# Weight sums on GpSimd and two residual chunks turned by DMA, in a two-layer decoder trunk

## The chip, the cores and the metric

One core of a Trainium2 chip runs one program. The metric is device time in microseconds (us) for one execution. The engines are named as the profile names them: PE is TensorE, DVE is VectorE, ACT is ScalarE, POOL is GpSimd and SP is SyncE, which here only starts DMAs. "L224" is line 224 of the kernel before the change.

## What is computed

Two layers over a residual stream `x` of 256 tokens by 2048 features in f32. Each layer has a mixer (differential attention in layer 0, latent attention in layer 1), a cross-attention into 256 memory tokens and a dense MLP. Each of them starts with an RMSNorm and ends with a plain add onto `x`.

```python
x = x + memory_cross_attention(rms_norm(x, cross_norm[i]), mem_h, ca_wq[i], ca_wkv[i], ca_wo[i])
x = x + sq_relu_mlp(rms_norm(x, mlp_norm[i]), mlp_wup[i], mlp_wdown[i])

def sq_relu_mlp(h, wup, wdown):        # wup 2048 x 8192, wdown 8192 x 2048
    return jnp.square(jax.nn.relu(h @ wup)) @ wdown
```

The change touches the two MLPs and the last step of each cross-attention, which feeds them.

## The kernel before the change

**Split weights.** Every f32 number is written as a high and a low part in the matmul's f32r format, and each product takes three matmuls: high by high, high by low, low by high. Activations stand still in the array and weights move through it, 512 columns at a time. A weight item is 1 MB (128 partitions by 2048 f32). It is loaded into one of seven buffers `raw`. Then it is split in two halves of 1024 columns: ACT casts the high part `whi` (L223), and DVE subtracts it to get the low part `wlo`, as `raw - whi` (L224). `whi` and `wlo` have four buffers each, so the split can be at most four halves ahead of PE.

**Blocks.** The 8192 hidden features fall into eight blocks of 1024. Block 0 of each MLP is computed plainly. Blocks 1 to 7 (the tuple `SEVEN`) are computed by class `Seven` with seven products p1 to p7 in place of eight: tokens, features and hidden columns are each cut in two, and sums of quarters of the activations are multiplied by sums of quarters of the weights. Each product has two items (`x` = 0 and 1), and an item of a product needs 12 matmuls, half of what an ordinary item needs (24, for both token halves). The order of the items in a block is p1 p1 p5 p5 p6 p3 p6 p3 p2 p7 p2 p7 p4 p4; at seven places in it an ordinary item of an earlier block's down-projection stands between them (`d` below): p1 p1 d p5 p5 d p6 d p3 p6 d p3 p2 d p7 p2 d p7 d p4 p4.

**Weight sums.** With quarters W11 to W22 of a block's weights, two buffers per `x` carry the running sums. `r["t", x]` is loaded with one quarter, and a DMA on POOL's queue that adds in flight (L961) puts W11 onto it when p1 runs. p1 itself uses W11 alone, p5 uses the sum. Before p6, DVE adds `r[22, x]` to it (L969, one instruction of 2048 columns). p3 uses `r[22, x]`; after its split a second adding DMA changes that buffer for p7. Before p2, DVE adds `r[21, x]` to `r["t", x]` (L969 again), which p4 uses last. So a block has four of these DVE adds, and the two MLPs have 56. A job's loads may be issued one job early: `fill` calls `fetch` of the job that is next in the plan.

**From the residual to the MLP.** `project_out` computes the cross-attention's output in four chunks of 512 features. For each chunk and token half, DVE adds the result onto `x` (L616), and `Forms.feed` makes the MLP's input from it: sum of squares (ACT), four 128x128 transposes on PE (`transpose4`, L176), multiplication by the norm's gain (DVE, L571), then a high and a low half (ACT L559, DVE L560). `FormUnit` tells PE's program which of these tasks an item waits for; before the change each unit waits for all tasks of its pair of chunks. The function `half_words` (ACT copy L392, store on POOL's queue L394) and `turned_by_dma` (DMA transpose on SP's queue, L399) are the other way to transpose, through DRAM; the norm ahead of each cross-attention uses it for chunks 0 and 1 already (`SENT`), as do the hidden blocks.

**Order of work.** PE's instructions stand in program order; the other engines' order is set by a planner in the compiler that simulates a timeline. `urgent()` gives work a higher priority in it, `behind(i)` puts an instruction after instruction `i`, and `keep_in_program_order` keeps DMAs in order. The helper tasks run on a clock of their own that counts PE's matmuls: a task's `yield T` means "go on when PE has worked T us more" (`T_SENT` 7.0, `T_BACK` 5.0, `T_ADD` 2.2).

Of the kernel before, what the change touches and what calls it, by code (L numbers as in the profile page):

```python
# [15 lines left out]
ALU = mybir.AluOpType  # L16
AX = mybir.AxisListType

P = 128
D = 2048  # L20
S = 256
NT = 2
CH = 512
# [5 lines left out]
SEVEN = (1, 2, 3, 4, 5, 6, 7)  # L29
# [5 lines left out]
T_EV, T_TURN, T_ROT, T_SM, T_SQ, T_ADD, T_NORM, T_SUM, T_BATCH, T_STORE, T_LAND, T_DMA, T_SHORT = 2.6, 2.6, 12.0, 6.5, 4.4, 2.2, 7.2, 3.0, 17.0, 22.0, 7.0, 8.0, 11.0  # L35

URGENT = 250
SENT = 0, 1
T_PART, T_JOIN, T_SENT, T_BACK = 5.0, 4.6, 7.0, 5.0
# [15 lines left out]
def trunk(ctx, tc, x, xT, xT0, mem, memT, positions, gcols, gfinal, lam_vecs, consts, W, out):  # L55
    nc = tc.nc
# [16 lines left out]
    def nm(s):  # L73
        serial[0] += 1
        return f"{s}_{serial[0]}"

    def unit():
        return units.tile([P, 2, 4, S], F32R, tag="unit", name=nm("unit"))
# [10 lines left out]
    class Task:  # L89
        def __init__(self, gen):  # L90
            self.gen = gen
            self.done = False
            self.waits = None
            self.ready = clock[0]
            self.serial = serial[0]
            side.append(self)
            self.step()
# [76 lines left out]
    def flip(o, src):  # L174
        clock[0] += 0.109
        nc.tensor.transpose(o, src, ident)  # L176

    def f32(ap):
        return ap.bitcast(F32)
# [3 lines left out]
    def behind(instruction):  # L183
        return tc.issue_after(instruction.ins) if instruction else nullcontext()

    def urgent():

        return tc.high_priority(offset=URGENT)
# [7 lines left out]
    def raw_tile():  # L196
        return wraw.tile([P, 4 * CH], F32, tag="raw", name=nm("raw"))
# [29 lines left out]
    def halves_of(raw, n=4 * CH, pieces=2):  # L227
        split = split_pieces(raw, n, pieces)
        for _ in range(pieces):
            split.next()  # L230
        return split.halves
# [158 lines left out]
    def half_words(src):  # L390
        planes = work.tile([P, 2, CH], U16, tag="ev", name=nm("planes"), padded_shape=[P, 2, CH], bufs=EVS)
        nc.scalar.copy(planes, src.bitcast(U16).rearrange("p (w s) -> p s w", s=2))  # L392
        there = turned.tile([2 * P, CH], U16, tag="turned", name=nm("turned"))
        nc.gpsimd.dma_start(there.rearrange("(q s) w -> q s w", s=2), planes)  # L394
        return there

    def turned_by_dma(there):
        landed = work.tile([P, 4, 2 * P], U16, tag="ev", name=nm("landed"), bufs=EVS)
        tc.keep_in_program_order(nc.sync.dma_start_transpose(landed, there))  # L399
        return landed.bitcast(F32).rearrange("p k t -> p k t")  # L400
# [29 lines left out]
    def transpose4(src, pt):  # L430

        for k in range(4):
            flip(pt[:, k * P : (k + 1) * P], src[:, k * P : (k + 1) * P])
        return pt.rearrange("p (k t) -> p k t", k=4)
# [25 lines left out]
    def sum_squares(acc, src, scale=1.0):  # L460
        junk = work.tile([P, CH], mybir.dt.bfloat16, tag="junk", name=nm("junk"), bufs=1)
        return nc.scalar.activation(junk[:, : src.shape[1]], src, AF.Square, scale=scale, accum_out=acc)  # L462
# [19 lines left out]
    class Stream:  # L482
# [8 lines left out]
        def feed(self, c, t, ps):  # L491
            if c not in self.units:
                self.units[c] = Held(unit())
            xc = xs[t][:, c * CH : (c + 1) * CH]

            def task():
                sum_squares(self.ss[t][:, c : c + 1], xc)
                yield T_ADD
                pt = transpose4(xc, ps)
                split(self.units[c], t, scaled(pt, g[:, self.gcol + 4 * c : self.gcol + 4 * c + 4]))  # L500
                yield T_TURN

            def unscaled():
                if c in self.sent:
                    with urgent():
                        there = half_words(xc)
                    yield T_SENT
                    pt = turned_by_dma(there)
                    yield T_BACK
                else:  # L510
                    yield T_ADD
                    pt = transpose4(xc, ps)
                split(self.units[c], t, pt)
                sum_squares(self.ss[t][:, c : c + 1], xc)
                yield T_TURN

            self.units[c].run(task() if self.sent is None else unscaled())
# [24 lines left out]
    class Forms(Stream):  # L542
# [2 lines left out]

        def __init__(self, gcol):
            super().__init__(gcol)
            self.raw = [raw_tile().rearrange("p (k t) -> p k t", t=P) for _ in range(NT)]
            self.forms = {}

# [11 lines left out]
        def feed(self, c, t, ps):  # L562
            xc = xs[t][:, c * CH : (c + 1) * CH]

            def task():
                sum_squares(self.ss[t][:, c : c + 1], xc)
                yield T_ADD
                pt = transpose4(xc, ps)
                rows = self.raw[t][:, 4 * c : 4 * c + 4]
                cols = g[:, self.gcol + 4 * c : self.gcol + 4 * c + 4]  # L570
                nc.vector.tensor_tensor(rows, pt, cols.unsqueeze(2).broadcast_to([P, 4, P]), ALU.mult)  # L571
                self.halves((t, c // 2), c % 2, rows)
                yield T_TURN

            self.form((t, c // 2)).run(task())

        def sum_of(self, key, inputs):

# [26 lines left out]
    class FormUnit:  # L605
        def __init__(self, forms, u):
            self.tiles = [forms.form((t, u // 2)) for t in range(NT)]
            self.at = 4 * (u % 2)
            self.tasks = [k for f in self.tiles for k in f.tasks]

        def get(self, half, kk, t):
            return self.tiles[t][:, half, self.at + kk]

    def add_residual(t, c, ps):
        xc = xs[t][:, c * CH : (c + 1) * CH]
        nc.vector.tensor_tensor(xc, xc, ps, ALU.add)  # L616


    def evacuate(ps, scale):
# [325 lines left out]
    class Seven:  # L945
# [20 lines left out]

        def job(self, p, x):
            def add(o, q):
                nc.vector.tensor_tensor(o, o, q, ALU.add)  # L969

            loads = {"p1": (("t", x), (0, 1)), "p6": ((22, x), (1, 1)), "p2": ((21, x), (1, 0))}

            def fetch():
                key, (i, j) = loads[p]
                if key not in self.raw:
                    home = f32(unit()).rearrange("p a k t -> p (a k t)") if p == "p1" and x == 0 and self.b < LAST - 2 else None
                    self.raw[key] = self.fetch(i, j, x, home=home)

            def run():
                r = self.raw  # L980
                if p in loads:
                    fetch()
                if p == "p1":
                    o = self.fetch(0, 0, x)
                    self.fetch(0, 0, x, r["t", x])
                elif p == "p5":
                    o = r["t", x]
                elif p == "p6":
                    o = r["t", x]
                    add(o, r[22, x])  # L990
                elif p == "p3":
                    o = r[22, x]
                    split = halves_of(o)
                    self.fetch(0, 1, x, o)
                    return split
                elif p == "p7":
                    o = r.pop((22, x))
                elif p == "p2":
                    o = r.pop((21, x))
                    add(r["t", x], o)  # L1000
                else:
                    o = r.pop(("t", x))
                return halves_of(o)

            if p in loads:
                run.fetch = fetch
            return run
# [260 lines left out]
    forms = {}  # L1268
# [45 lines left out]
    rows = ahead[:, 16 : 16 + 4 * S].rearrange("p (k t) -> p k t", t=S)  # L1314
# [144 lines left out]
    def project_out(acts_o, gcol):  # L1459
        nxt = Forms(gcol)  # L1460
        for c in range(4):
            ps = matmul_chunk(acts_o)
            for t in range(NT):
                add_residual(t, c, ps[t])
                nxt.feed(c, t, ps[t])
        return nxt

    def project_group(o, nxt=None, each=None):
        for c in range(4):
            ps = matmul_chunk([o])  # L1470
            if each:
                each(c)
            for t in range(NT):
                add_residual(t, c, ps[t])
                if nxt:
                    nxt.feed(c, t, ps[t])
# [248 lines left out]
    ps = matmul_chunk(acts, LAT)  # L1725
    latent_piece(eq, 0, ps, 0, LAT)
    ps = matmul_chunk(acts, LAT)
# [4 lines left out]
    ps = matmul_chunk(acts, 320)  # L1732
# [272 lines left out]
```

## Time and profile before the change

| What | Value |
|---|---|
| Time, median of 3 runs | 2160.42 us (2160.02 to 2160.5) |
| The profiled execution's own time | 2159.85 us |
| Its span, first to last instruction | 2158.1 us |
| PE busy | 2147.1 us, 99% |
| DVE busy | 1733.3 us, 80% |
| ACT busy | 1486.7 us, 69% |
| POOL busy | 225.4 us, 10% |
| Granted TensorE clock | 0.999 |

The span begins with the first instruction and ends with the last; the execution's own time has 1.75 us more around it. In a row of the groups, the numbers are the count, the busy time in us, the mean of one in ns, and the idle time of the engine just before such instructions with what ended it. In a row of the timeline they are the start, the length (of all instructions merged into the row) and how many there are.

### The profile page before, as it was taken

The page shows a single profiled execution, that of the slowest core. Times are in us where ns is not written, and L with a number is a line of the kernel's source. Part 1 is how long each engine was busy: PE and PEld are TensorE (multiplying, and loading weights), DVE is VectorE, ACT ScalarE, POOL GpSimd, SP SyncE. Part 2 cuts the span into 40 slices and gives each one's busy share as a digit, 9 for nine tenths or more (in the row PEclk, how much of TensorE's full clock was granted, in tenths as well). Part 3 has the DMA queues.
Part 4 walks back from the last instruction along what each step waited for, and adds up shares of the span by engine and source line. Part 5 has one row for each costly group of instructions (what it writes and reads, how often), then busy time and mean ns, then how long its engine had stood idle before and what let it go on. Part 6 is the DMA issues. An engine that isn't in the chain of part 4 may idle for free.

```text
span 2158.1 us, 27532 instructions
## 1 busy us (share of the span) xinstructions
PE 2147.1 (99%) x10109; PEld 1796.9 (83%) x10109; DVE 1733.3 (80%) x1962; ACT 1486.7 (69%) x1978; POOL 225.4 (10%) x354
## 2 busy tenths in 40 slices
PE   9999999999999999999999999999999999999998
PEld 7888888888888888888889988888888888888887
DVE  6576878788888889788886878778888888888887
ACT  7576656767777777776665765666777777777665
POOL 1123210001000000000000420000000000000001
PEclk9999999999999999999999999999999999999999
DMA  9678796748999999998986464665999999999995
GB/s 386 207 232 282 226 296 220 234 156 267 295 292 259 312 283 254 318 277 265 305 250 217 135 202 159 225 220 179 289 295 290 266 308 285 268 279 309 261 315 146
DMA packets 173944, 553.72 MB, mean 257 GB/s; under 512 B 100464, under 2 KB 100848, under 8 KB 114928
## 3 DMA queue, kind: packets, MB, share of 16 engines
q1 hardware_dynamic: 155136, 445.26, 58.6%
q0 software_dynamic: 18240, 105.92, 23.2%
q8 instruction: 79, 1.29, 0.2%
q10 hardware_dynamic: 432, 0.79, 0.1%
q14 instruction: 57, 0.47, 0.1%
HBM read 505.38 MB, written 24.12 MB: 245 GB/s over the span
## 4 chain that ended last, share of the span: by engine, by line
PE 96%; DVE 2%; DMA 1%; issue 1%; ACT 0%; DVEq 0%; POOLq 0%; POOL 0%
PE mm L172 63%; PE pr L172 28%; PE ax L172 3%; DMA raw<-in_mlp_wup_dram 1%; PE ax L176 1%; DVE wlo L224 1%; PE mm L176 1%; DVE raw L969 0%; DVE x L616 0%; DVE unit L428 0%; ACT whi L223 0%; PE ax L1326 0%; PE pr L176 0%; DVE unit L382 0%; DVE x L1875 0%
## 5 line engine op out<-in xcount | busy, mean ns | idle before, releaser
L224 DVE TENSOR_TENSOR wlo<-raw,whi 128x1024 fp32r<-128x1024 f32 (+3 forms) x930 | 1118.8, 1216 | 321.2 <-ACT whi L223 299.1
L223 ACT CAST whi<-raw 128x1024 fp32r<-128x1024 f32 (+3 forms) x929 | 968.2, 1044 | 541.6 <-PE mm L172 381.1
L172 PE MATMUL mm<-whi,unit 128*128 128x512 f32 (+2 forms) x4000 | 1268.9, 389 | 0.3
L172 PEld LDWEIGHTS mm<-whi,unit 128*128 128x128 f32 x4000 | 749.0, 188 | 148.9 <-DVE unit L382 1.1
L172 PE MATMUL mm<-wlo,unit 128*128 128x512 f32 (+2 forms) x2000 | 773.8, 387 | 0.2
L172 PE MATMUL pr<-whi,unit 128*128 128x512 f32 x1912 | 610.0, 389 | 0.0
L172 PEld LDWEIGHTS mm<-wlo,unit 128*128 128x128 f32 x2000 | 376.3, 188 | 73.6 <-DVE wlo L224 3.2
L172 PEld LDWEIGHTS pr<-whi,unit 128*128 128x128 f32 x1912 | 358.6, 188 | 73.4
L172 PE MATMUL pr<-wlo,unit 128*128 128x512 f32 x956 | 371.8, 389 | 0.4 <-DVE wlo L224 0.4
L172 PEld LDWEIGHTS pr<-wlo,unit 128*128 128x128 f32 x956 | 179.5, 188 | 39.2 <-DVE wlo L224 2.4
L394 POOL DMA_DIRECT2D turned<-planes x84 | 47.6, 567 | 732.2 <-ACT planes L392 706.6
L969 DVE TENSOR_TENSOR raw<-raw,raw 128x2048 f32<-128x2048 f32 x40 | 91.5, 2288 | 9.0 <-DMA raw<-in_mlp_wup_dram 8.8
L616 DVE TENSOR_TENSOR x<-x,mm 128x512 f32<-128x512 f32 x128 | 85.2, 682 | 15.2 <-PE mm L172 15.1
L961 POOL DMA_DIRECT2D raw<-in_mlp_wup_dram x48 | 43.4, 905 | 448.0 <-DVE wlo L224 425.7
L468 POOL TENSOR_TENSOR rs<-rs,mhalf 128x1 f32<-128x1 f32 (+1 forms) x26 | 21.7, 837 | 385.7 <-DVE rs L467 385.6
L224 DVE TENSOR_TENSOR wlo<-unit,whi 128x1024 fp32r<-128x1024 f32 x48 | 57.3, 1221 | 5.3 <-ACT whi L223 4.0
L223 ACT CAST whi<-unit 128x1024 fp32r<-128x1024 f32 x48 | 49.8, 1054 | 9.8 <-PE pr L172 9.8
L392 ACT COPY planes<-p 128x1024 uint16<-128x1024 uint16 x48 | 50.0, 1041 | 0.3
L172 PE MATMUL mm<-unit,whi 128*128 128x256 f32 x256 | 46.7, 284 | 0.0
L462 ACT ACTIVATE junk<-x 128x512 bf16<-128x512 f32 (+1 forms) x57 | 35.3, 619 | 11.0 <-DVE x L1174 5.2
L1539 ACT ACTIVATE p<-p,r 128x512 f32<-128x512 f32 x42 | 30.4, 724 | 15.3 <-DVE p L1044 7.4
L172 PEld LDWEIGHTS mm<-unit,whi 128*128 128x128 f32 x256 | 40.2, 192 | 0.3
(207 smaller groups left out, 1314.3 us busy)
## 6 DMA issues: line engine op xcount, KB each, us to landing
raw<-in_mlp_wdown_dram SPq DMA_DIRECT2D x128, 1024.0 KB, 7.2
raw<-in_mlp_wup_dram SPq DMA_DIRECT2D x120, 1024.0 KB, 7.0
raw<-in_mlp_wup_dram POOLq DMA_DIRECT2D x48, 1024.0 KB, 9.0
raw<-in_da_wqkv_dram SPq DMA_DIRECT2D x45, 1024.0 KB, 8.6
turned<-planes POOLq DMA_DIRECT2D x84, 256.0 KB, 6.1
raw<-in_da_wo_dram SPq DMA_DIRECT2D x16, 1024.0 KB, 8.2
raw<-in_ca_wkv_dram SPq DMA_DIRECT2D x16, 1024.0 KB, 7.6
raw<-in_mlp_wdown_dram POOLq DMA_DIRECT2D x16, 1024.0 KB, 10.2
```

The costliest lines, as they stand in the source:

```text
L172: return nc.tensor.matmul(o, stationary, moving, start=start, stop=stop, skip_group_check=onto)
L176: nc.tensor.transpose(o, src, ident)
L223: nc.scalar.copy(hi, r)
L224: nc.vector.tensor_tensor(lo, r, f32(hi), ALU.subtract)
L392: nc.scalar.copy(planes, src.bitcast(U16).rearrange("p (w s) -> p s w", s=2))
L394: nc.gpsimd.dma_start(there.rearrange("(q s) w -> q s w", s=2), planes)
L462: return nc.scalar.activation(junk[:, : src.shape[1]], src, AF.Square, scale=scale, accum_out=acc)
L468: nc.gpsimd.tensor_tensor(r[:, :n], r[:, :n], mhalf.broadcast_to([P, n]), ALU.pow)
L616: nc.vector.tensor_tensor(xc, xc, ps, ALU.add)
L961: tc.keep_in_program_order(nc.gpsimd.dma_start(onto, src, accum_op=ALU.add))
L969: nc.vector.tensor_tensor(o, o, q, ALU.add)
L1539: nc.scalar.activation(r, src, AF.Relu, scale=rstd[t])
```

## The change

Part 1 moves the weight sums. `add` goes from DVE, in one instruction of 2048 columns, to GpSimd, in two of 1024. The sum ahead of p6 is issued when the quarter `r[22, x]` is fetched, one job earlier than before. In the first block that uses the seven products (block 1 of each MLP), the sum for p5 is no longer made by an adding DMA from DRAM; GpSimd adds the W11 that p1 has loaded anyway.

Part 2 concerns the residual chunks 0 and 1 ahead of each MLP. They are transposed through DRAM in place of PE, with an order hint that keeps the multiplication by the gain behind the latest residual add, and `FormUnit` waits only for its own chunk's tasks.

```diff
@@ class Forms @@
+            self.turning = {}
@@ feed @@
             def task():
+                if c in SENT:
+                    with urgent():
+                        there = half_words(xc)
                 sum_squares(self.ss[t][:, c : c + 1], xc)
-                yield T_ADD
-                pt = transpose4(xc, ps)
+                if c in SENT:
+                    yield T_SENT
+                    pt = turned_by_dma(there)
+                    yield T_BACK
+                else:
+                    yield T_ADD
+                    pt = transpose4(xc, ps)
                 rows = self.raw[t][:, 4 * c : 4 * c + 4]
                 cols = g[:, self.gcol + 4 * c : self.gcol + 4 * c + 4]
-                nc.vector.tensor_tensor(rows, pt, cols.unsqueeze(2).broadcast_to([P, 4, P]), ALU.mult)
+                with behind(c in SENT and latest[0]):
+                    nc.vector.tensor_tensor(rows, pt, cols.unsqueeze(2).broadcast_to([P, 4, P]), ALU.mult)
                 self.halves((t, c // 2), c % 2, rows)
                 yield T_TURN

-            self.form((t, c // 2)).run(task())
+            form = self.form((t, c // 2)).run(task())
+            self.turning[t, c] = form.tasks[-1]
@@ class FormUnit @@
-            self.tasks = [k for f in self.tiles for k in f.tasks]
+            self.tasks = [forms.turning[t, u] for t in range(NT)]
@@ add_residual @@
-        nc.vector.tensor_tensor(xc, xc, ps, ALU.add)
+        latest[0] = nc.vector.tensor_tensor(xc, xc, ps, ALU.add)
@@ Seven.job @@
             def add(o, q):
-                nc.vector.tensor_tensor(o, o, q, ALU.add)
+                for at in (slice(0, 2 * CH), slice(2 * CH, 4 * CH)):
+                    nc.gpsimd.tensor_tensor(o[:, at], o[:, at], q[:, at], ALU.add)
@@ fetch @@
                     self.raw[key] = self.fetch(i, j, x, home=home)
+                    if p == "p6":
+                        add(self.raw["t", x], self.raw[22, x])
@@ run @@
                 if p == "p1":
                     o = self.fetch(0, 0, x)
-                    self.fetch(0, 0, x, r["t", x])
+                    if self.b == SEVEN[0]:
+                        add(r["t", x], o)
+                    else:
+                        self.fetch(0, 0, x, r["t", x])
...
                 elif p == "p6":
                     o = r["t", x]
-                    add(o, r[22, x])
```

More of the change, by code (lines that the diff above doesn't have):

```diff
@@ L608, in __init__ @@
             self.at = 4 * (u % 2)
-            self.tasks = [k for f in self.tiles for k in f.tasks]
+            self.tasks = [forms.turning[t, u] for t in range(NT)]
         def get(self, half, kk, t):
             return self.tiles[t][:, half, self.at + kk]
+    latest = [None]
     def add_residual(t, c, ps):
         xc = xs[t][:, c * CH : (c + 1) * CH]
-        nc.vector.tensor_tensor(xc, xc, ps, ALU.add)
+        latest[0] = nc.vector.tensor_tensor(xc, xc, ps, ALU.add)
     def evacuate(ps, scale):
```

## The prediction

> **What bounds the kernel now.** First the page: engine shares and the chain that ended last, then the DVE groups with shapes kept apart, then the waits of PE's weight loads.
>
> ```profile
> span 2158.1 us, 27532 instructions
> PE 2147.1 (99%) x10109; PEld 1796.9 (83%) x10109; DVE 1733.3 (80%) x1962; ACT 1486.7 (69%) x1978; POOL 225.4 (10%) x354
> PE 96%; DVE 2%; DMA 1%; issue 1%; ACT 0%; DVEq 0%; POOLq 0%; POOL 0%
> ```
> ```profile
> L969 DVE TENSOR_TENSOR raw<-raw,raw 128x2048 f32<-128x2048 f32 x40 | 91.5, 2288 | 9.0 <-DMA raw<-in_mlp_wup_dram 8.8
> L969 DVE TENSOR_TENSOR unit<-unit,raw 128x2048 f32<-128x2048 f32 x16 | 36.6, 2288 | 0.8 <-DMA raw<-in_mlp_wup_dram 0.6
> ```
> ```profile
> PEld mm L172 <- DVE wlo L224: 3.2, 8, 0.5
> PEld pr L172 <- DVE wlo L224: 2.4, 5, 0.6
> ```
>
> PE is the bound: it idles 2158.1 - 2147.1 = 11.0 us in all, and its loads waited 3.2 + 2.4 = 5.6 us for DVE's low parts. So a time below this one can come only from work taken off PE, or from those few us. The 56 sums hold DVE for 91.5 + 36.6 = 128 us, yet PE hardly waits for it. What decides about part 1 is thus not DVE's share but how far the splits run ahead of PE. That is seen in one block of layer 1: PE's side from the chain in order of time, DVE's and ACT's from the timeline.
>
> ```profile
> 1582.72 2.72 PE pr L172 x12
> ...
> 1607.20 5.44 PE pr L172 x24
> 1612.64 5.44 PE mm L172 x24
> 1618.08 2.72 PE pr L172 x12
> 1620.80 5.44 PE mm L172 x24
> 1626.24 5.44 PE pr L172 x24
> 1631.68 5.44 PE mm L172 x24
> 1637.12 5.44 PE pr L172 x24
> ```
> ```profile
> 1602.33 2.36 DVE L224 TENSOR_TENSOR wlo<-unit,whi 128x1024 fp32r<-128x1024 f32 x2 [0.67 <-ACT whi L223]
> 1604.72 2.29 DVE L969 TENSOR_TENSOR unit<-unit,raw 128x2048 f32<-128x2048 f32 x1
> 1606.93 1.22 DVE L224 TENSOR_TENSOR wlo<-raw,whi 128x1024 fp32r<-128x1024 f32 x1
> 1608.32 2.59 DVE L224 TENSOR_TENSOR wlo<-raw,whi 128x1024 fp32r<-128x1024 f32 x2 [0.17 <-ACT whi L223]
> 1610.82 2.28 DVE L969 TENSOR_TENSOR raw<-raw,raw 128x2048 f32<-128x2048 f32 x1
> 1613.02 1.22 DVE L224 TENSOR_TENSOR wlo<-raw,whi 128x1024 fp32r<-128x1024 f32 x1
> ...
> 1625.78 2.28 DVE L969 TENSOR_TENSOR unit<-unit,raw 128x2048 f32<-128x2048 f32 x1
> 1627.98 3.49 DVE L224 TENSOR_TENSOR wlo<-raw,whi 128x1024 fp32r<-128x1024 f32 x3
> 1631.38 2.29 DVE L969 TENSOR_TENSOR raw<-raw,raw 128x2048 f32<-128x2048 f32 x1
> ...
> 1637.66 2.36 DVE L224 TENSOR_TENSOR wlo<-raw,whi 128x1024 fp32r<-128x1024 f32 x2
> ```
> ```profile
> 1611.31 1.05 ACT L223 CAST whi<-unit 128x1024 fp32r<-128x1024 f32 x1 [0.30 <-PE pr L172]
> ```
>
> A product's item is 2.72 us on PE (12 matmuls), a `d` item 5.44, a block 14 x 2.72 + 7 x 5.44 = 76.2 us. A half of a product's item is 1.36 us on PE, and its low part 1.13 us on DVE (three in 3.49, the last of them 1.22). ACT waits for PE to give a buffer back, so the splits cannot run further ahead than the four buffers. PE's row at 1607.20 is p5 p5, 1612.64 `d`, 1618.08 p6, 1620.80 `d`, 1626.24 p3 p6, 1631.68 `d`, 1637.12 p3 p2. The pair of low parts at 1637.66 is p2's: the first ends near 1638.8 and PE wants it at 1639.84 plus one matmul, 1640.1, so only 1.3 us is in hand. For p6's second half (the second low part of a product after 1625.78, done at 1629.2, wanted at 1630.5) it is also 1.3 us.
>
> **Part 1: the sums on POOL.** Removed: 56 DVE instructions of 2.29 us. Added: 60 sums (56, and two in each MLP's first block) of two instructions each, 120 on POOL. The trace of before has the same form at a quarter of the width, once with DVE beside it, and smaller ones in layer 1's mixer:
>
> ```profile
> 2135.95 3.46 DVE L224 TENSOR_TENSOR wlo<-raw,whi 128x1024 fp32r<-128x1024 f32 x2
> 2136.34 1.99 POOL L1896 TENSOR_TENSOR x<-x,unit 128x512 f32<-128x512 f32 x1 [17.56 <-ACT junk L462]
> ```
> ```profile
> 1200.75 0.46 POOL L635 TENSOR_TENSOR rope<-ev,sin 128x128 f32<-128x128 f32 x1
> ```
> ```profile
> 1200.77 1.52 DVE L224 TENSOR_TENSOR wlo<-raw,whi 128x1024 fp32r<-128x1024 f32 x1 [0.30 <-ACT whi L223]
> ```
>
> Two low parts that follow each other take 2.36 us at 1602.33 and 3.46 us here: 1.10 us longer, next to a POOL instruction that began 0.39 us into the first of them and ran 1.99. The reading that fits: POOL waited 0.8 us for the first low part to end, then ran 1.15 us while the second stood still. At 1200.77 one low part took 1.52 in place of 1.22 beside a 128x128 one of 0.46. So the two engines exclude each other, and 384 more columns cost 1.10 - 0.30 = 0.80 us, 2.1 ns each. A half sum of 1024 columns then holds DVE for 1.10 + 512 x 2.1 ns = 2.2 us, the whole sum for 4.4, against 2.2 that DVE spent itself (2.29 less the overlap). **The change does not free DVE; it takes 2.2 us more of its time per sum.** The lower end for a half is 2.0 us (with 3.46 - 2 x 1.22 = 1.02 in place of 1.10), the upper end 4.0 (twice the whole 1.99). No exclusion at all at this width is one of the rivals, since no row shows 1024 columns.
>
> The Trainium skill, "SBUF — State Buffer", section "Who interferes with whom", has the rule: a DVE instruction with two SBUF inputs contends with a GpSimd instruction that reads SBUF, and whoever starts first has the port for the whole instruction. The 1.10 us above agree; by that rule DVE's residual adds, with one input in PSUM, would go on beside a sum, and the sum below would come out lower by what share of them meets one. The "GPSIMD Engine Reference", section "Elementwise — side-by-side cycle accounting", gives 4497 ns for an add of 2048 f32, so 2.25 us for a half by that page, which would put 0.1 us more on each sum and some 4 us on the forecast.
>
> What lies in the lead and what reaches PE, walked through the block above. p6's first sum can start when p5's split is done, at 1604.7. POOL 1604.7 to 1606.9; low part 1606.9 to 1608.1, as before; POOL 1608.1 to 1610.3; low part to 1611.4, wanted at 1611.5. The next one, for `d`, runs to 1612.5 (wanted 1612.8). p6's second sum has been ready since 1611.4: POOL to 1614.7, low part to 1615.8, wanted at 1615.6, PE is 0.2 late; POOL to 1618.0, low part of p6 to 1619.1, wanted at 1618.3 + 0.2, 0.6 later still. The p6 pair costs PE 0.8 us. In the p2 pair each sum costs 2.2 us more than before where 1.3 was in hand: 0.9 each, 1.8. Together 2.6 us a block; 14 blocks give 36 us. Between the ends: nothing, if lead recovered elsewhere covers it, and 56 x 2.2 = 123 us, if all the excess reaches PE. I take the walk.
>
> The sums themselves arrive in time: 4.4 us plus two waits of 1.2 is 6.8 us, and the pieces they feed come later (p6's cast at 1611.31 needs only the first half, done at 1606.9; p2's pair at 1637.66 is 11.9 us after its sum's old start). Behind a waiting sum on POOL's queue stand the stores for the hidden blocks and p3's adding DMA.
>
> ```profile
> L961 POOL DMA_DIRECT2D raw<-in_mlp_wup_dram x48: 863/887/1261, 487.2 to 2016.9; - x48
> ...
>   ACT whi L223: 9.4, 5
> ...
> DMA to landing us min/median/max: 7.9/9.5/17.5
> ```
>
> Those adding DMAs were waited for 9.4 us in all; p3's lands 7.9 to 17.5 us after its issue, and p7's split comes an item or two later still. I cost the delay at nothing; without that cover it would be up to 6.8 us for a DMA, and the time would go to the third rival's. In an MLP's first block, two sums of 4.4 us come on top where an adding DMA cost DVE nothing: 2 x 4.4 against leads of 1.3 to 2.6; I take 2 us per MLP, 4 in all, ends 0 and 18. Four adding DMAs (and 4 MB) go, worth at most those 9.4 us, and by count 4 in 48 of them, 0.8: nothing.
>
> **Part 2: chunks 0 and 1 by DMA.** PE loses 2 chunks x 2 halves x 4 transposes = 16 per MLP. Their price is the distance of two chunks in the chain: 6.33 us, with 24 matmuls of 5.44 in it.
>
> ```profile
> 462.40 5.46 PE mm L172 x24
> 468.73 5.49 PE mm L172 x24
> ```
>
> Eight transposes cost 6.33 - 5.44 = 0.89 us; four times that, 3.6 us, leaves PE's own time and so the path. Added: 8 ACT copies, 8 stores on POOL, 8 transposing DMAs on SP. The same path in the cross-attention ahead shows what it costs:
>
> ```profile
> 399.31 0.39 PE L172 MATMUL mm<-wlo,unit 128*128 128x512 f32 x1
> 399.84 0.73 PE L172 MATMUL mm<-whi,unit 128*128 128x512 f32 x2
> ```
> ```profile
>   PEld mm L172: 0.6, 1
> ...
> DMA to landing us min/median/max: 3.3/3.3/4.7
> ```
> ```profile
> 455.00:482.00 27.00, 27.00 (x137) 22.68 (x136) 22.87 (x33) 18.86 (x32) 0.00 (x0) 1.00 0.52 189
> ```
>
> There the first unit is wanted three chunks after its rows were added, as here, and PE was 0.3 us late once (399.84 against 399.54). The stretch ahead of the MLP has its DMAs at 0.52 and ACT busy 18.9 of 27.0 us, so four copies near 1 us fit. If that cover were gone, SP's transposes would wait and hold up the weight loads behind them. I take 0.3 us per MLP, 0.6; ends 0 and 3 each.
>
> **Sum.** 2159.85 (this execution) - 3.6 + 36 + 4 + 0.6 = 2196.9; the runs' median is 0.57 above this execution, so 2197.4, +1.7%.
>
> **The rivals.** *The excess is absorbed* (the other side): DVE is idle a fifth of the span, and if the planner or the wait for p2's quarter moves the POOL halves next to `d` items, whose halves are 2.72 us on PE, the lead covers them. It decides where less than 1.3 us of a sum's excess falls between two product items. Then only part 2 counts: 2160.42 - 3.6 + 0.6 = 2157.4, -0.14%. For it: PE waited 5.6 us in all so far. Against it: 1.3 us in hand, 2.2 taken. *The engines do not exclude each other at this width*: DVE gains 128 us, the 5.6 us of waits go too: 2157.4 - 5.6 = 2151.8, -0.4%. Against it are the 3.46 and 1.52 us rows. *The delays pile up*: each late half moves the next sum into a shorter lead, and nothing is won back; twice the walk, 5.2 us a block: 2197.4 + 36 + 4 = 2237. That the change does less than it says is no case here: 16 transposes go in each MLP whatever else happens.
>
> **Chances and range.** The walk or a like size 0.57, piled up 0.20, absorbed 0.14, no exclusion 0.09. About 0.2% (4.3 us) is what a measurement of this kernel can tell from no change. Absorbed falls mostly within it (0.11 of 0.14, the rest faster): faster 0.12, same 0.11, slower 0.77. The walk's own range is 2175 to 2222 (1.2 to 4 us a block). Leaving out 0.09 below and about 0.1 above, the range is 2156 to 2238.
>
> **What would show it.** POOL's sums at 2.2 to 3.5 us each and low parts (L224) with a mean above 1.23 us, many near 3.4; waits of PE's loads for L224 grown from 5.6 to about 40 us, mostly at p6, p3 and p2; PE busy down 3.6 us in transposes; no wait for `landed` at the MLPs' start over 1 us. If L224 keeps its mean, the exclusion is wrong; if it grows and PE does not wait, the lead was larger than I read.

## The result and the profile after

| | before | after |
|---|---|---|
| Time, median | 2160.46 us (2160.02 to 2160.71) | 2271.01 us (2269.36 to 2273.0) |
| Ratio | | 1.0513, 95% interval 1.0498 to 1.0527 |
| Profiled execution | 2159.85 us | 2269.89 us (span 2268.1) |

The change made the kernel 110.6 us slower. The forecast was 2197.4 us, with a range up to 2238: the direction was right, the size was not. The page of the changed kernel, with the rows that answer to those of before (L983 is the sum, on POOL now):

```profile
span 2268.1 us, 27674 instructions
PE 2179.0 (96%) x10077; PEld 1791.6 (79%) x10077; DVE 1839.9 (81%) x1906; ACT 1492.1 (66%) x1986; POOL 590.7 (26%) x478
PE 72%; DVE 16%; issue 7%; ACT 2%; DMA 2%; SPq 0%; POOL 0%; DVEq 0%; POOLq 0%; ACTq 0%
L224 DVE TENSOR_TENSOR wlo<-raw,whi 128x1024 fp32r<-128x1024 f32 (+3 forms) x930 | 1329.7, 1446 | 330.7 <-ACT whi L223 312.4
L983 POOL TENSOR_TENSOR raw<-raw,raw 128x1024 f32<-128x1024 f32 x84 | 263.2, 3170 | 38.4 <-DMA raw<-in_mlp_wup_dram 23.3
L983 POOL TENSOR_TENSOR unit<-unit,raw 128x1024 f32<-128x1024 f32 x36 | 106.0, 3012 | 56.8 <-DMA raw<-in_mlp_wup_dram 35.5
```

The low parts' row of before reads:

```profile
L224 DVE TENSOR_TENSOR wlo<-raw,whi 128x1024 fp32r<-128x1024 f32 (+3 forms) x930 | 1118.8, 1216 | 321.2 <-ACT whi L223 299.1
```

DVE lost 128 us of sums and is still busy 106.6 us longer, because its low parts stretched (1329.7 - 1118.8 = 211 us). The chain that ended last gives PE 72% in place of 96%, and DVE 16% in place of 2%; in the block shown below its longer pieces of "issue" lie inside low parts that stand still. The waits of PE's weight loads say the same; before, the first two rows were 3.2 and 2.4 us:

```profile
PEld mm L172 <- DVE wlo L224: 70.9, 59, 4.3
PEld pr L172 <- DVE wlo L224: 41.7, 42, 2.3
PEld mm L172 <- DVE unit L561: 6.5, 3, 2.7
```

By the distances between the first matmuls of successive p1 products, a regular block took 76.16 us before and 83.2 after. Against before, 46.0 us are lost in MLP 0's seven blocks and 46.7 in MLP 1's. The stretches ahead of the two MLPs' first such block lost 7.9 and 9.5 more.

One block of layer 1 shows how. From the timelines of DVE, POOL and PE (a row of DVE or POOL merges instructions that follow each other, with their count at the end):

```profile
1675.77 2.42 DVE L224 TENSOR_TENSOR wlo<-raw,whi 128x1024 fp32r<-128x1024 f32 x1 [0.91 <-ACT whi L223]
1678.49 9.72 DVE L224 TENSOR_TENSOR wlo<-raw,whi 128x1024 fp32r<-128x1024 f32 x3 [0.30 <-ACT whi L223]
...
1697.66 16.30 DVE L224 TENSOR_TENSOR wlo<-raw,whi 128x1024 fp32r<-128x1024 f32 x6 [1.54 <-ACT whi L223]
```
```profile
1673.81 6.65 POOL L983 TENSOR_TENSOR unit<-unit,raw 128x1024 f32<-128x1024 f32 x2 [1.34 <-DVE wlo L224]
1680.42 6.71 POOL L983 TENSOR_TENSOR raw<-raw,raw 128x1024 f32<-128x1024 f32 x2
1697.11 0.89 POOL L974 DMA_DIRECT2D raw<-in_mlp_wup_dram  x1 [9.98 <-issue]
1697.73 5.05 POOL L983 TENSOR_TENSOR unit<-unit,raw 128x1024 f32<-128x1024 f32 x2
1703.95 6.66 POOL L983 TENSOR_TENSOR raw<-raw,raw 128x1024 f32<-128x1024 f32 x2 [1.17 <-DVE wlo L224]
```
```profile
1684.92 0.50 PE L172 MATMUL mm<-wlo,unit 128*128 128x512 f32 x1 [1.68 <-DVE wlo L224]
1688.27 0.50 PE L172 MATMUL mm<-wlo,unit 128*128 128x512 f32 x1 [0.31 <-DVE wlo L224]
1703.92 0.50 PE L172 MATMUL pr<-wlo,unit 128*128 128x512 f32 x1 [1.76 <-DVE wlo L224]
1708.40 0.50 PE L172 MATMUL mm<-wlo,unit 128*128 128x512 f32 x1 [1.44 <-DVE wlo L224]
1711.75 0.50 PE L172 MATMUL mm<-wlo,unit 128*128 128x512 f32 x1 [0.31 <-DVE wlo L224]
```

p6's two sums (1673.81 and 1680.42) run without a gap: four halves, 3.3 us each. Beside them the three low parts at 1678.49 need 9.72 us, one per 3.2 us, where they took 3.49 before; PE wants one per 1.36 us in a product and per 2.72 us in a `d` item. In p2's first sum (1697.73) both halves take 5.05 us together, not 6.7: DVE got no turn between them, and the low part that began at 1697.66 ended at 1703.87, 6.2 us later. p2's second sum goes in turns again. PE stood 1.68 + 0.31 us behind p6's pair and 1.76 + 1.44 + 0.31 us behind p2's, 5.5 us. The distances of the matmuls' starts are the better measure, since the matmul after a wait is followed 0.34 us later in place of 0.23: by them the two pairs cost 2.8 and 4.4 us, nearly all of the 7.3 us by which this block is longer. In 10 of the 14 blocks p2's first sum goes as it does here; in the first and the last of each MLP's seven it goes in turns.

### The profile page after: what moved, and what is told of

The parts are those of the page before. It is cut to its first block, busy times and chain, and to the rows that moved or that the text cites. A ratio compares the mean times of both kernels' runs of the same rounds, so it can differ in the third digit from the quotient of the medians.

```text
span 2268.1 us, 27674 instructions
## 1 busy us (share of the span) xinstructions
PE 2179.0 (96%) x10077; PEld 1791.6 (79%) x10077; DVE 1839.9 (81%) x1906; ACT 1492.1 (66%) x1986; POOL 590.7 (26%) x478
## 4 chain that ended last, share of the span: by engine, by line
PE 72%; DVE 16%; issue 7%; ACT 2%; DMA 2%; SPq 0%; POOL 0%; DVEq 0%; POOLq 0%; ACTq 0%
PE mm L172 49%; PE pr L172 20%; DVE wlo L224 12%; PE ax L172 2%; ACT whi L223 1%; DMA landed<-turned 1%; DVE unit L561 1%; PE ax L176 1%; DVE x L629 1%; DVE raw L599 1%; DVE raw L581 0%; DVE unit L382 0%; DVE wlo L243 0%; ACT planes L392 0%; PE mm L176 0%
## 5 line engine op out<-in xcount | busy, mean ns | idle before, releaser
L224 DVE TENSOR_TENSOR wlo<-raw,whi 128x1024 fp32r<-128x1024 f32 (+3 forms) x930 | 1329.7, 1446 | 330.7 <-ACT whi L223 312.4
L223 ACT CAST whi<-raw 128x1024 fp32r<-128x1024 f32 (+3 forms) x929 | 967.4, 1043 | 581.7 <-PE mm L172 398.1
L172 PE MATMUL mm<-wlo,unit 128*128 128x512 f32 (+2 forms) x2000 | 782.8, 392 | 46.8 <-DVE wlo L224 46.1
L172 PE MATMUL pr<-wlo,unit 128*128 128x512 f32 x956 | 376.5, 394 | 24.8 <-DVE wlo L224 24.7
L983 POOL TENSOR_TENSOR raw<-raw,raw 128x1024 f32<-128x1024 f32 x84 | 263.2, 3170 | 38.4 <-DMA raw<-in_mlp_wup_dram 23.3
L394 POOL DMA_DIRECT2D turned<-planes x92 | 52.2, 567 | 795.8 <-ACT planes L392 780.4
L983 POOL TENSOR_TENSOR unit<-unit,raw 128x1024 f32<-128x1024 f32 x36 | 106.0, 3012 | 56.8 <-DMA raw<-in_mlp_wup_dram 35.5
L224 DVE TENSOR_TENSOR wlo<-unit,whi 128x1024 fp32r<-128x1024 f32 x48 | 57.2, 1218 | 5.6 <-ACT whi L223 5.5
L1103 POOL DMA_DIRECT2D raw<-in_mlp_wdown_dram x16 | 13.9, 872 | 170.8 <-DVE wlo L224 134.6
L223 ACT CAST whi<-unit 128x1024 fp32r<-128x1024 f32 x48 | 49.6, 1051 | 13.3 <-PE pr L172 13.3
L172 PE MATMUL mm<-unit,whi 128*128 128x256 f32 x256 | 46.7, 284 | 0.0
```

Source lines behind the costliest of these rows:

```text
L172: return nc.tensor.matmul(o, stationary, moving, start=start, stop=stop, skip_group_check=onto)
L223: nc.scalar.copy(hi, r)
L224: nc.vector.tensor_tensor(lo, r, f32(hi), ALU.subtract)
L983: nc.gpsimd.tensor_tensor(o[:, at], o[:, at], q[:, at], ALU.add)
```

## The experiments

All changes are against the kernel before, unless said. Ratios are against runs of the kernel before on the same chip.

### The two parts alone

Part 1 alone is the diff's `Seven.job`; part 2 alone is the rest.

> Part 1 alone on the kernel before (sums on GpSimd, the first block's sum too; all residual chunks still turned on PE). Theory (GpSimd's sums hold DVE's two-input work): the blocks cost as much as in the changed kernel, about 93 us, and some 5 us more come ahead of the first blocks, 2255 to 2262 us. Rival (the two parts hurt each other, mainly at the MLPs' starts): under 2240 us.

> Part 2 alone on the kernel before (chunks 0 and 1 turned by DMA, sums on DVE). By the prediction's own step: -3.6 + 0.6, 2157.5 us. By what the changed kernel's trace shows ahead of its MLPs (PE waits 2.4 and 0.9 us for the last chunks' rows, and the matmuls behind a long wait run at 427 ns): 2160 to 2168 us.

Part 1 alone: 2265.07 us, 1.0484 (1.0467 to 1.0502). Part 2 alone: 2166.12 us, 1.0029 (1.0018 to 1.004). Some 105 us come from the sums, 3 us more than the range expected, and 6 from the residual chunks, and they add up. Part 2 was meant to gain 3.6 us; 32 matmuls are gone from PE's count, yet the time rose. Waits of PE in part 2 alone, and SP's queue at MLP 0's start in the changed kernel:

```profile
PE mm L172 <- DVE unit L561: 4.5, 2, 2.2
```
```profile
463.71 3.48 SPq L399 DMA_TRANSPOSE landed<-turned  x2
467.24 0.59 SPq L191 DMA_DIRECT2D unit<-in_mlp_wup_dram  x1
467.92 0.46 SPq L191 DMA_DIRECT2D raw<-in_mlp_wup_dram  x1
468.92 8.40 SPq L399 DMA_TRANSPOSE landed<-turned  x2
```

Chunk 0's two transposes hold SP 3.5 us, chunk 1's 8.4; two weight loads were issued between them. The rows of chunk 1 arrive late. From issue to landing, the four transposes took:

```profile
DMA to landing us min/median/max: 3.3/3.8/9.9
```

The 9.9 us are those of chunk 1's first transpose, issued at 468.92; of the four stores ahead of them, chunk 1's second took 8.1 us and the others 2.3 to 3.4. At MLP 1's start the stores took at most 4.2 us, the slowest transpose 10.2, and PE waited 2.2 us all the same. The weight loads behind chunk 1's transposes on SP wait with them until 477.4. Sending chunk 0 alone tells whether it is chunk 1 (the change is against part 2 alone):

```diff
+SENT_MLP = (0,)
-                if c in SENT:          # the three places in feed
+                if c in SENT_MLP:
```

> Part 2 alone, with chunk 0 alone turned by DMA: 8 transposes less per MLP, and the rows that came late in the changed kernel (chunk 1's, 2.4 us) are turned on PE again. Theory (part 2 loses by chunk 1 coming late and SP's queue standing behind its transposes): 2156 to 2161 us. Rival (any DMA transpose there costs): 2163 us or more.

2159.96 us, 0.9995 (0.9986 to 1.0004): the loss is chunk 1's. The half of the saving that is left, 1.8 us, is under what can be measured here. That the two 1 MB loads are what delays chunk 1's transposes was not tried.

### The engine, the tie, or the port

First the changed kernel with its sums put back on DVE, everything else kept (`nc.gpsimd` to `nc.vector` in `add`, still in halves).

> The changed kernel with its sums on DVE again, but still in two halves, issued early for p6, and the first block's sum still made on chip. Theory (the engine is what costs): the blocks return to the times of before, 2158 to 2170 us, what part 2 alone gives plus at most 5. Rival (the early issue, the halves or the sum in place of the adding DMA is what costs): over 2200 us.

2178.69 us, 1.0087 (1.0072 to 1.0102). The engine alone costs 2271.0 - 2178.7 = 92 us. The time is 9 us above what was expected and 12.6 above part 2 alone: 2.9 of it lie ahead of MLP 0's blocks, 4.4 and 3.8 within the two MLPs' blocks, most of that in the first and the last two. Sums issued early stand ahead of low parts on DVE too; this was not followed further.

Then two theories of why GpSimd costs it. Either splits wait for sums that GpSimd makes slowly, or the two engines exclude each other. In the first kernel below the splits of p6, p2 and p4 take buffers that no sum writes, so the sums run with nobody waiting for them. In the second, GpSimd writes zeros over the same places instead of adding. Both kernels leave the sums out of the products.

```diff
 # part 1, p6 / p2 / p4
-                    o = r["t", x]
+                    o = r[22, x]
-                    o = r.pop((21, x))
+                    o = r[21, x]
-                    o = r.pop(("t", x))
+                    r.pop(("t", x)); o = r.pop((21, x))
 # second kernel, besides
-                    nc.gpsimd.tensor_tensor(o[:, at], o[:, at], q[:, at], ALU.add)
+                    nc.gpsimd.memset(o[:, at], 0.0)
```

> Part 1 alone, but no split waits for a sum: p6 splits the quarter W22 and p4 the quarter W21 in place of the sums, so the result of the sums is left out of the products, while GpSimd makes all 120 of them at the same places. Theory (the sums hold DVE's other work): as slow as part 1 alone, within 10 us. Rival (the splits come late because a sum takes GpSimd 6.7 us in place of DVE's 2.3): within 15 us of the kernel before, under 2176 us.

> As the run in which no split waits for a sum, but GpSimd's 120 additions are 120 memsets onto the same halves, in the same places of its queue: it writes and reads nothing. The sums are left out. Theory (what holds DVE is GpSimd reading SBUF while DVE reads two inputs): the low parts keep their 1.22 us, 2150 to 2165 us. Rival (any work of GpSimd on SBUF, or its place in the queue, holds DVE): over 2200 us.

Untied: 2287.31 us, 1.0589 (1.0573 to 1.0605), 22 us more than part 1 and not less; within 10 us had been expected. Its longest low part stood 10.6 us, which is four halves and its own run: with nothing to wait for, GpSimd ran both sums of p2's pair without giving DVE a turn, in six of the 14 blocks. With zeros: 2156.29 us, 0.9978 (0.9969 to 0.9987). The groups of that kernel:

```profile
L224 DVE TENSOR_TENSOR wlo<-raw,whi 128x1024 fp32r<-128x1024 f32 (+3 forms) x962 | 1165.5, 1217 | 437.1 <-ACT whi L223 400.0
L970 POOL MEMSET raw<- 128x1024 f32 x84 | 78.2, 952 | 41.6 <-DMA raw<-in_mlp_wup_dram 20.5
L970 POOL MEMSET unit<- 128x1024 f32 x36 | 33.8, 956 | 117.1 <-DMA unit<-in_mlp_wup_dram 100.2
```

120 GpSimd instructions at the same places leave L224 at 1217 ns, and a regular block has its 76.16 us again. Not latency, then, but the exclusion of the two engines, and an instruction that only writes takes no part in it. A memset is 0.95 us where a half sum holds about 2.25, so the size of the effect is not compared at equal length; but no trace of stretching is left. This kernel also shows what freeing DVE of all 128 us of sums is worth here: 4.6 us. The Trainium skill, "SBUF — State Buffer", section "Who interferes with whom", says that a DVE instruction with two SBUF inputs contends with a GpSimd instruction that reads SBUF and not with one that only writes. These two runs agree.

### The size of a piece

Part 1 with each sum in one, four or eight instructions in place of two:

```diff
-                for at in (slice(0, 2 * CH), slice(2 * CH, 4 * CH)):
+                for at in (slice(i * W, (i + 1) * W) for i in range(4 * CH // W)):   # W = 2048, 512, 256
```

> Part 1 alone with each sum as one instruction of 2048 columns: DVE stands still 4.5 us at a time. Theory (turns): worse than with halves, 2275 to 2310 us. Rival (only the total counts): 2255 to 2275 us.

> Part 1 alone with each sum in four pieces of 512 columns. The port time is the same (4 x 1.1 us a sum), but DVE gets a turn after each 1.1 us in place of 2.25, so a low part every 2.3 us in place of 3.4 while sums run, against 1.4 to 2.7 that PE wants. Theory (PE stalls because four halves come in a row with one low part between): 2195 to 2235 us. Rival (only the total time of the port counts): 2255 to 2275 us, as with halves.

> The additions on GpSimd alone (part 1), each sum in eight instructions of 256 elements a lane. Theory of turns: while both engines have work, they alternate instruction by instruction, and VectorE waits for one GpSimd instruction at most each time; the series of one, two and four pieces (2290, 2265, 2237 us) goes on falling, to 2185 to 2225 us. Rival, the total that GpSimd holds counts and not its pieces: more instructions bring their own starts, 2240 to 2275 us.

| Pieces of a sum | Time, us | Ratio | Longest low part, us |
|---|---|---|---|
| 1 x 2048 | 2290.42 | 1.0599 (1.0581 to 1.0616) | 5.9 |
| 2 x 1024 (part 1) | 2265.07 | 1.0484 (1.0467 to 1.0502) | 6.0 |
| 4 x 512 | 2236.82 | 1.0359 (1.0333 to 1.0385) | 8.0 |
| 8 x 256 | 2253.33 | 1.0432 (1.0416 to 1.0447) | 9.1 |

Up to four pieces the time falls as the theory of turns has it (four came out 2 us above its range): DVE waits for one GpSimd instruction at a time, and a smaller one holds it less. With eight it rises again. The theory of turns gave 2185 to 2225 and missed; the rival's range, 2240 to 2275, held the time, but by the total alone it would not have fallen from one to four. The timeline of POOL, the chain and the timeline of PE in the eight-piece kernel show what else happens:

```profile
1681.30 0.89 POOL L961 DMA_DIRECT2D raw<-in_mlp_wup_dram  x1
1681.91 5.81 POOL L970 TENSOR_TENSOR unit<-unit,raw 128x256 f32<-128x256 f32 x8
1687.44 2.98 POOL L970 TENSOR_TENSOR raw<-raw,raw 128x256 f32<-128x256 f32 x4
1691.59 5.00 POOL L970 TENSOR_TENSOR raw<-raw,raw 128x256 f32<-128x256 f32 x3 [1.17 <-DVE wlo L224]
```
```profile
1682.47 9.05 DVE wlo L224
```
```profile
1691.57 0.80 PE L172 MATMUL pr<-wlo,unit 128*128 128x512 f32 x1 [6.22 <-DVE wlo L224]
```

Twelve pieces ran 0.69 us apart, and the low part that began at 1682.47 stood through all of them. It ended only when GpSimd itself had to wait for that low part (the row at 1691.59, 1.17 us). In the same block, where the pieces alternate with low parts, one takes 1.67 us (the last row, three in 5.00). So there are two ways to share: in turns, one instruction each, or GpSimd keeping the port for as long as it has work ready. Ten low parts stood over 4.5 us in this kernel, as did ten in part 1. Of the 63.2 us that PE's matmuls waited for low parts here, 51 came straight behind these ten. Two rivals stay beside this for the rise from four pieces to eight: eight pieces 0.69 us apart hold DVE for 5.5 us a sum where four, 1.25 us apart, hold it for 5.0, and ACT's casts waited 45.5 us for sums that came late, in place of 8.7 with four pieces.

What can be read of which way it goes: where GpSimd kept the port in these rows and in the block shown of the changed kernel, it came from its own queue with no wait for DVE (here, and in the other block at 1697.11, it had just issued a DMA), and each instruction began 0.35 us before the one ahead of it ended; in turns it began 0.04 us before. In the changed kernel this divides all the sums: the ten whose first half follows straight on a DMA's issue kept the port, the 50 others took turns. It is not enough by itself, for with four pieces only four of ten such sums kept it; in the six others a low part had begun 0.7 us ahead of the first piece. What makes the hardware choose was not isolated.

### Which sums

Part 1 split up: p6's sums alone, p2's sums alone (the others stay on DVE in one instruction, p1's first-block sums on the adding DMA), and all but the first block's.

```diff
 # p6 alone: add(..., nc.gpsimd) in fetch, add on nc.vector for p2
 # p2 alone: add(..., nc.gpsimd) for p2, add on nc.vector for p6 at its old place
 # part 1 without the first block's
-                    if self.b == SEVEN[0]:
-                        add(r["t", x], o)
-                    else:
-                        self.fetch(0, 0, x, r["t", x])
+                    self.fetch(0, 0, x, r["t", x])
```

> The kernel before, with p6's two sums of a block alone on GpSimd, in halves and issued early; p2's sums and the first block's stay as before. By the stalls in the trace of the changed kernel (2.06 and 0.31 us behind p6's pair), 2.3 to 2.8 us a block times 14: 2192 to 2212 us. By the walk of the prediction, 0.8 us a block: 2168 to 2175 us. If the sums count by the time they hold, whichever product they belong to, half of the excess of part 1: 2205 to 2215 us.

> The kernel before, with p2's two sums of a block alone on GpSimd, in halves; p6's sums and the first block's stay as before. By the stalls in the trace of the changed kernel (1.65, 1.62 and 0.47 us in p2), 3.7 to 4.2 us a block times 14: 2212 to 2225 us. By the walk of the prediction, 1.8 us a block: 2182 to 2190 us.

> The additions on GpSimd alone (part 1), but p1's sums of an MLP's first block made by the adding DMA, as before. In the changed kernel each first block takes 5 to 6 us more than the blocks behind it have lost, and activation sums beside p1's additions take 2.9 us in place of 0.7: 10 to 15 us under part 1 alone, 2248 to 2257 us. If the start of an MLP is late for another reason (the accumulated products' places), 2262 to 2267 us.

| On GpSimd | Time, us | Ratio | Over before, us |
|---|---|---|---|
| p6's sums | 2194.18 | 1.0158 (1.0142 to 1.0173) | 33.6 |
| p2's sums | 2209.87 | 1.0228 (1.0213 to 1.0244) | 49.3 |
| both | 2248.63 | 1.0405 (1.0388 to 1.0423) | 88.1 |
| both and the first block's | 2265.07 | 1.0484 (1.0467 to 1.0502) | 105.2 |

The pairs cost 2.4 and 3.5 us a block (33.6 / 14 and 49.3 / 14). The stalls in the trace gave 2.3 to 2.8, which holds, and 3.7 to 4.2, 0.2 more than was measured. That a sum costs by the time that it holds, whichever product it belongs to (2205 to 2215 for p6's), fell. Together the pairs cost 88.1 us, 5.2 more than apart. The first block's sums cost 2265.07 - 2248.63 = 16.4 us (17.1 by the last column), some 8 per MLP. p6's kernel has no low part over 4.5 us, p2's has ten, of 5.7 to 5.9 us: p6's sums take turns, p2's first sum keeps the port in ten blocks of 14.

## Why the prediction was wrong

**Right: the exclusion and its price.** The step said that a half sum holds DVE for 2.2 us and that the change takes DVE time rather than freeing it. In the changed kernel the shortest half takes 2.40 us, one that waits for a low part 3.37 to 3.43, which less the low part's 1.13 is 2.25 to 2.3. That is also the 2.25 us estimated beside it from the "GPSIMD Engine Reference" of the Trainium skill, section "Elementwise — side-by-side cycle accounting". The rival without exclusion (2151.8) fell with it. The reading from two short rows of before, 3.46 and 1.52 us, held at twice the width of the larger one. The residual adds, which have one input in PSUM, keep their length, though twelve of them run beside a sum (before, then after):

```profile
L616 DVE TENSOR_TENSOR x<-x,mm x128: 667/682/690, 333.5 to 2146.7; 128x512 f32<-128x512 f32 x128
L629 DVE TENSOR_TENSOR x<-x,mm x128: 664/679/692, 333.7 to 2256.7; 128x512 f32<-128x512 f32 x128
```

That is as the prediction's rule from "SBUF — State Buffer" in the Trainium skill, section "Who interferes with whom", had it.

**Wrong: the walk.** The step that failed is the order of turns in "The next one, for `d`, runs to 1612.5" and "p6's second sum has been ready since 1611.4: POOL to 1614.7". I let DVE do two low parts in a row although a GpSimd instruction was waiting, and so put the first sum's delay behind DVE's lead before the second began. The trace has GpSimd's next half start as soon as one low part is done: four halves in a row with one low part between each. The p6 pair cost 2.4 us where the walk had 0.8. The same walk with that turn given to GpSimd comes to it: GpSimd 1611.4 to 1613.6, the low part for `d` to 1614.7 (wanted 1612.8, 1.9 late), GpSimd to 1616.9, the next low part to 1618.0 (wanted 1615.6 + 1.9, 0.5 later still), 2.4 in all.

The p2 pair failed by the same sentence twice: "each sum costs 2.2 us more than before where 1.3 was in hand: 0.9 each" charges each sum against a full lead. After the first sum there is no lead left for the second (0.9 + 2.2 = 3.1), and in the first sum DVE mostly did not even get its turn between the halves. It cost 3.5 us where the walk had 1.8. Both pairs: 2.6 us a block foreseen, 6.3 measured with both on GpSimd, 88 us in place of 36.

**Wrong: p1's sums in the first block**, 2 us per MLP taken, some 8 measured; it lies inside the ends given, 0 and 18 for both. My step set these sums against low parts only. At an MLP's start DVE also makes activation sums, which have two SBUF inputs too. From DVE's timeline of the changed kernel:

```profile
486.92 2.29 DVE L561 TENSOR_TENSOR unit<-raw,unit 128x512 fp32r<-128x512 f32 x1
489.13 0.68 DVE L599 TENSOR_TENSOR raw<-raw,raw 128x512 f32<-128x512 f32 x1
489.73 2.89 DVE L561 TENSOR_TENSOR unit<-raw,unit 128x512 fp32r<-128x512 f32 x1
...
493.74 2.88 DVE L599 TENSOR_TENSOR raw<-raw,raw 128x512 f32<-128x512 f32 x1
```

An instruction of 0.68 us takes 2.3 to 2.9 beside a half sum, and PE waits there for both kinds. (The adding DMAs, counted there as 48, are 56, for eight go onto `unit` buffers; that changes nothing.)

**Wrong: part 2.** -3.6 + 0.6 was foreseen, +6.2 measured. The 16 transposes per MLP went, as said. The step that failed is "the first unit is wanted three chunks after its rows were added, as here", taken from the cross-attention's landing times of 3.3 to 4.7 us. These are its transposes alone; its stores took 2.3 to 7.3 us in the same stretch. Chunk 0 kept to the cover; chunk 1's slowest transposes needed 9.9 and 10.2 us, and one of its stores 8.1. "If that cover were gone, SP's transposes would wait and hold up the weight loads behind them" is what happened.

**Right: sums in time.** The delay of the sums themselves was costed at nothing; in the changed kernel no cast (L223) waits for a sum of GpSimd, and the run with nobody waiting for them was no faster.

**The rivals.** "The delays pile up" came nearest to the mechanism: "each late half moves the next sum into a shorter lead, and nothing is won back". It did not have the port kept over several instructions. Its price, twice the walk, gave 2237; the measured 88 us of the pairs, 16 of the first blocks and 6 of part 2 give 2160.5 + 88 + 16 + 6 = 2270.5. These terms are differences of runs, so the sum tests only that the two parts add up. "Absorbed" fell: of 2.2 us per sum, 88 / 56 = 1.6 reached PE. The walk's upper end, 123 us if all of it did, was the bound that held the time. The range left it out, and should not have: the p2 pair has two sums in one lead of 1.3 us, which one can count in the block of before without any walk.

**The signs named ahead.** Half sums of 2.2 to 3.5 us: 3.1 in the mean. L224 above 1.23: 1.446. Waits of PE's loads up to about 40: 112.6. PE's transposes: 32 matmuls fewer, but PE's busy time, named to fall by 3.6 us, rose by 31.9; what makes up this rise was not followed. No wait for landed rows over 1 us: 2.2 in each MLP, for the units made of them.

## What to carry to other kernels

Before work goes from DVE to an idle GpSimd, count the inputs: if both engines then read two SBUF operands at once, the work is not moved but made twice as dear, and DVE stands while it runs. When pricing it, put all GpSimd instructions of a burst in a row, with at most one DVE instruction between two of them and perhaps none, and charge the whole burst against one lead. A gain of a few us from work taken off the bounding engine can be lost when the data it now waits for comes by a queue that also carries the weight loads.

## What was not expected of the hardware

**A waiting DVE instruction can be passed over many times.** 6.2 us with two halves, 9.05 with twelve pieces of 256, 10.6 with four halves that nothing stops. The Trainium skill, "SBUF — State Buffer", section "Who interferes with whom", says of DVE's two-port modes that whoever issues first has the shared pair for the whole instruction. These rows show that GpSimd can have it for several.

**PE runs at half rate after some of these waits.** From PE's timeline, at MLP 1's start in the changed kernel:

```profile
1566.23 0.50 PE L172 MATMUL mm<-wlo,unit 128*128 128x512 f32 x1 [3.87 <-DVE wlo L224]
...
1567.80 0.63 PE L172 MATMUL mm<-wlo,unit 128*128 128x512 f32 x1
1568.23 1.05 PE L172 MATMUL mm<-whi,unit 128*128 128x512 f32 x2
```

From 1567.80 the matmuls start 0.43 us apart in place of 0.227, and the trace's granted clock is 0.50 from 1568 to 1570. The changed kernel has 47 such starts where the kernel before has 13. 39 of them stand in six stretches behind waits of 1.8 to 3.9 us, but two waits of 2.2 us were followed by none; 34 x 0.2 us is 7 of the 110. The kernel with eight pieces has 100. The Trainium skill, "TensorE: Matmul & The Clock Gate", section "Part 1: The HAM clock gate (the "warmup" mystery)", has PE at half clock after an idle window of about 3.4 us that runs freely. Here only one of the six waits was that long, the others 1.8 to 2.4 us; which waits do it was not tried.
